# Differential attention in a two-block network: the work behind a tile's scores cut into three pieces that run over four steps

## The chip, the cores and the metric

The kernel runs on one core of a Trainium2 chip. The metric is the device time of one execution in microseconds. Everything is float32; the dense matrix products split each operand into a rounded high part and the rest (dtype `fp32r`) and take three products for one.

## The reference, cut to what matters

Two blocks of two layers each act on 512 tokens of width 1024 (the second block also on 256 context tokens). The part that the change touches is the differential attention of the second block, in both of its layers: 4 heads, two softmax maps per head over 768 keys (512 of the sequence, 256 of the context), subtracted with a learned factor, times the values, then a norm over each head.

```python
def diff_softmax_attend(q, keys, vals, lam):
    s = jnp.einsum('bqhmd,bkhmd->bhmqk', q, keys).astype(jnp.float32) * (DA_QK ** -0.5)
    p = jax.nn.softmax(s, axis=-1)
    w = p[:, :, 0] - lam * p[:, :, 1]
    return jnp.einsum('bhqk,bkhv->bqhv', w.astype(vals.dtype), vals)
...
def diff_out(o):
    return (rms_norm(o, da_subln) * (1.0 - lam_init)).reshape(o.shape[:2] + (DA_WIDTH,))
yl = jnp.concatenate([hgrn_out(ol_f + ol_b, pl[2]), diff_out(od_l).astype(hl.dtype),
                      fourier_mix(pl[8])], axis=-1) @ w_out
```

In the first of the two layers the context tokens attend too, over the 256 context keys alone; in the second only the 512 sequence tokens do. So a head has 6 query tiles of 128 tokens in layer 0 (two of them context tiles) and 4 in layer 1: 24 + 16 = 40 tiles of a head.

## The kernel before

The program is written for a tile framework. It tracks dependences between tiles, gives each tag of a pool a number of buffers, and puts the instructions of each engine into a fixed order when it compiles: the order in which the program issues them is the priority, but an instruction that the compiler finds not ready is passed by later ones. On the chip each engine works through that fixed order and waits where something is late.

`mixer` is the sequence mixer of a layer. Its last stage is the differential attention, loop over heads `h` and tiles `c` (`order`), with dense work spread in between. The dense work comes from a `Filler`: a chain of generators (projections of the second pair of heads, the gate projection, the Fourier branch, half of the output projection) that `fill.step(cols)` advances by about `cols` columns of matrix product (512 columns are one dense product). A step takes `DA_COLS` = 8000 (layer 0) or 7500 (layer 1) columns.

For each tile the program has two pieces:

- `diff_front` (L1418): for both maps, scores on TensorE into a PSUM tile `at` (L1431; 512 + 256 columns for a sequence tile, 256 for a context tile), row minimum on VectorE (L1434), exponential with row sum on ScalarE into a buffer `P` (L1436), then the two small terms (L1440, L1441) and the combined weights, written into the first map's buffer, on VectorE (L1442).
- `diff_back` (L1445): transposes of the combined weights on TensorE into PSUM tiles `tp`, 6 for a sequence tile (L1453); copies to `wT` on ScalarE, two for a sequence tile (L1454); the products with the values (L1460), two key blocks side by side in the array; a copy to `o2` on ScalarE (L1463); a small product with a stacked identity that adds the two halves (L1464); a scaled copy into `od` on ScalarE (L1465). Plain float32 products appear in the trace as two instructions each, so L1460 has 12 for a sequence tile and L1464 has 2.

A step of the loop issues `diff_front` of tile i, then `fill.step(DA_COLS[l])`, then `diff_back` of tile i-1. Tiles of the last head also get `attn_out` (L1603: square, reduce, norm, transposes L1588, split into the output projection's operands) one step after their `diff_back`. After the loop come three `fill.step(DA_LAST)` with the last pieces between them.

PSUM has 8 banks here: `acc` (dense products) 2 tiles of one bank, `tp` 2 tiles of one bank, `at` 2 tiles of two banks. `tp` is shared by the transposes, the value products, the Fourier branch (L1546) and L1588. `wT` and `o2` have 2 buffers, `P` has 5, `ard` (the factor 1/sum) 6 by its pool's default. The evacuation of a gate product is `gfn` (L1517: tanh on ScalarE L1519, product on VectorE L1520, product on GpSimd L1521). Weights come by DMA and are split by `wsplit` into `hi` on ScalarE (L288) and `lo` on VectorE (L289). The dense products are L301, L302, L305 (`mm_a_g`) and L321 to L323 (`mm_b_g`).

Of the kernel before, what the change touches and what calls it, by code (L numbers as in the profile page):

```python
# [9 lines left out]
F32 = mybir.dt.float32  # L10
# [3 lines left out]
AF = mybir.ActivationFunctionType  # L14
# [12 lines left out]
DA_COLS = (8000, 7500)  # L27
# [4 lines left out]
DA_LAST = 5832  # L32
DA_FIRST = 9540
# [218 lines left out]
class Builder:  # L252
# [1165 lines left out]
    def diff_front(self, p, l, maps, c):  # L1418

        nc = self.nc  # L1420
        N = T + CT
        k0 = 0 if c < 4 else T
        nk = N - k0
        P = []
        den = self.t(self.small, [128, 2], F32, "aden")
        for m in range(2):
            QS, KS = maps[m]
            ps = self.t(self.ps, [128, 1024], F32, "at")
            for o in range(k0, N, 512):
                n = min(512, N - o)  # L1430
                nc.tensor.matmul(ps[:, o - k0:o - k0 + n], lhsT=QS[:, 128 * c:128 * c + 128], rhs=KS[:, o:o + n],  # L1431
                                 start=True, stop=True)
            mx = self.t(self.small, [128, 1], F32, "amx")
            nc.vector.tensor_reduce(mx, ps[:, :nk], AX.X, ALU.min)  # L1434
            e = self.t(p, [128, N], F32, "P", NP)
            nc.scalar.activation(out=e[:, :nk], in_=ps[:, :nk], func=AF.Exp, scale=-1.0, bias=mx, accum_out=den[:, m:m + 1])  # L1436
            P.append(e)

        rd = self.t(self.small, [128, 2], F32, "ard")
        nc.vector.reciprocal(rd, den)  # L1440
        nc.vector.scalar_tensor_tensor(rd[:, 1:2], den[:, 0:1], self.lam[:, l:l + 1], rd[:, 1:2], ALU.mult, ALU.mult)  # L1441
        nc.vector.scalar_tensor_tensor(P[0][:, :nk], P[1][:, :nk], rd[:, 1:2], P[0][:, :nk], ALU.mult, ALU.add)  # L1442
        return P[0], rd, k0, nk

    def diff_back(self, p, h, c, front, dv, od):  # L1445
        nc = self.nc
        W, rd, k0, nk = front
        wT = self.t(p, [128, T + CT], F32, "wT", 2)
        for o in range(0, nk, 512):
            n = min(512, nk - o)  # L1450
            pt = self.t(self.ps, [128, 512], F32, "tp")
            for i in range(0, n, 128):
                nc.tensor.transpose(pt[:, i:i + 128], W[:, o + i:o + i + 128], self.ident)  # L1453
            nc.scalar.copy(wT[:, o:o + n], pt[:, :n])  # L1454

        po = self.t(self.ps, [128, 192], F32, "tp")
        nb = nk // 128
        for i in range(nb):
            g = 64 * (i % 2)
            nc.tensor.matmul(po[g:g + 64, :128], lhsT=dv[:, k0 // 128 + i, 64 * h:64 * h + 64], rhs=wT[:, 128 * i:128 * i + 128],  # L1460
                             start=(i < 2), stop=(i >= nb - 2), tile_position=(0, g))
        o2 = self.t(p, [128, 128], F32, "o2", 2)
        nc.scalar.copy(o2, po[:, :128])  # L1463
        nc.tensor.matmul(po[:, 128:], lhsT=o2, rhs=self.ident2, start=True, stop=True)  # L1464
        nc.scalar.activation(out=od[:, c, 64 * h:64 * h + 64], in_=po[:, 128:], func=AF.Copy, scale=rd[:, 0:1])  # L1465

    def mixer(self, l, hp, hT, hc, vx, vt, fill):

        nc, tc, A = self.nc, self.tc, self.A
        both = self.segs(hT, hc)  # L1470
        qseg = both if l == 0 else both[:1]
        W = A["wi_a"][l]
        nt = 6 if l == 0 else 4
        NQ = 128 * nt
# [3 lines left out]
        dv = self.t(mx, [128, 6, 256], F32, "dv")  # L1478

        ha, hb = ExitStack(), ExitStack()  # L1480
        if vt is None:
            vt, fill = self.scan_values(l, self.pool(vx, f"vx{l}", side="right"), both)
# [11 lines left out]
        fill = Filler(dense[1])  # L1494
        chains = {0: self.hgrn_chain(hg[0], hg[1], l, 0, vt, oh, NQ, *st[0])}
        h = 1
        while chains:
            for i, g in list(chains.items()):
                if next(g, "end") == "end":
                    chains.pop(i)  # L1500
                    if i == 2:
# [4 lines left out]
                        prep = [self.diff_prep(dp, W, both, NQ, j) for j in range(2)]  # L1506
# [8 lines left out]
        da = self.pool(ctx, f"da{l}")  # L1515
# [9 lines left out]
        br = {}  # L1525
# [77 lines left out]
        def attn_out(c):  # L1603
# [8 lines left out]

        fill = Filler(prep[1], self.dense_b_g([(A["wi_g"][l, i], (2, 512)) for i in range(4)], self.tok_tiles(qseg), gfn),
                      fourier(), out_half())
        pend = []
        for h in range(4):
            if h == 0:
                stacks = [self.diff_stack(da, i, NQ) for i in range(2)]
                fill.step(DA_FIRST)
            elif h < 3:  # L1620
                while fill.gens and fill.gens[0] is prep[1]:
                    fill.step(512)
                stacks.append(self.diff_stack(da, h + 1, NQ))
            maps = stacks[h]
            for c in order:
                fr = self.diff_front(da, l, maps, c)
                fill.step(DA_COLS[l])
                if pend:
                    self.diff_back(da, *pend[-1], dv, od)
                if h == 3 and len(pend) > 3 * nt + 1:  # L1630
                    while "l" not in br or (l == 0 and "c" not in br):
                        fill.step(512)
                    attn_out(pend[-2][1])
                pend.append((h, c, fr))
        fill.step(DA_LAST)
        self.diff_back(da, *pend[-1], dv, od)
        fill.step(DA_LAST)
        attn_out(order[-2])
        fill.step(DA_LAST)
        attn_out(order[-1])  # L1640
        fill.drain()
        brT, brc = br["l"], br.get("c")
        ctx.close()
# [309 lines left out]
```

## Time and profile before

| | |
|---|---|
| median of 3 runs | 2590.91 us (2587.81 to 2595.76) |
| the profiled execution, its own time | 2587.33 us |
| its span from first to last instruction | 2585.5 us |
| TensorE busy | 2511.3 us, 97% of the span |
| mean granted clock of TensorE | 0.993 |
| differential attention with its dense work, layer 0 | 1049 to 1205 us of the span |
| the same, layer 1 | 2043 to 2157 us of the span |

The profile is one execution. The span lies 1.8 us under that execution's own time, and that time 3.6 us under the median of the runs. PE is TensorE's matrix products, PEld its weight loads, which overlap them; DVE is VectorE, ACT ScalarE, POOL GpSimd. An engine's busy time is the union of its instructions; the products of PE are pipelined and overlap their neighbours, so the pace of PE is read from start to start, not from durations.

### The profile page before, as it was taken

Reading aid. Unit: us, or ns where it says so; the run is one execution under the profiler, and the core shown is the slowest. Engines: PE = TensorE matmul, PEld = TensorE weight load, DVE = VectorE, ACT = ScalarE, POOL = GpSimd, SP = SyncE. Lnnn points to the kernel's source line nnn. Section 1 sums busy time; section 2 is a strip of 40 time slices with the busy share of each in tenths; the row PEclk is TensorE's granted clock in tenths of the full one; section 3 lists DMA queues with packets and bytes.
Section 4 is the critical chain, followed back from the end, with each engine's and each line's share of the span. In section 5 each row is a group of like instructions: output and inputs, shape, how many; then the busy total and the mean of one; then the engine's idle time right before and its main releaser. Section 6 shows DMA issues by size and latency. Waiting matters only on the chain.

```text
span 2585.5 us, 38643 instructions
## 1 busy us (share of the span) xinstructions
PE 2511.3 (97%) x15587; PEld 2071.2 (80%) x15587; DVE 1516.8 (59%) x2502; ACT 1031.9 (40%) x1962; POOL 241.7 (9%) x288
## 2 busy tenths in 40 slices
PE   8999999999999999999999999999999999999997
PEld 7777887787777888777988888888788777887886
DVE  5657588645365577666756544445567766443434
ACT  6523333333444544465631211212655466522222
POOL 0000012102000000512100000000100412000001
PEclk9999999999999999999999999999999999999999
DMA  5424364342131211522543333332211434322222
GB/s 187 159 73 162 107 228 131 98 131 74 58 130 66 82 34 53 146 81 101 190 146 123 131 122 105 127 120 90 90 58 50 120 110 147 115 91 97 91 97 81
DMA packets 85169, 284.63 MB, mean 110 GB/s; under 512 B 12176, under 2 KB 15072, under 8 KB 84608
## 3 DMA queue, kind: packets, MB, share of 16 engines
q1 hardware_dynamic: 78880, 263.50, 30.0%
q0 software_dynamic: 4864, 15.74, 2.2%
q10 hardware_dynamic: 1248, 2.95, 0.4%
q8 instruction: 122, 2.00, 0.3%
q14 instruction: 55, 0.45, 0.1%
HBM read 253.78 MB, written 21.00 MB: 106 GB/s over the span
## 4 chain that ended last, share of the span: by engine, by line
PE 77%; DVE 7%; issue 5%; ACT 5%; DMA 3%; POOL 2%; SPq 0%; DVEq 0%; POOLq 0%; ACTq 0%
PE acc L301 13%; PE acc L305 13%; PE acc L302 13%; PE acc L321 9%; PE acc L323 9%; PE acc L322 9%; DVE lo L289 2%; ACT hi L288 1%; PE tp L1460 1%; PE at L1431 1%; DMA raw<-in_wo 1%; PE tp L1453 1%; ACT junk L344 1%; ACT hf L388 1%; PE at L650 1%
## 5 line engine op out<-in xcount | busy, mean ns | idle before, releaser
L289 DVE TENSOR_TENSOR lo<-raw,hi 128x1024 fp32r<-128x1024 f32 (+1 forms) x321 | 388.0, 1211 | 400.0 <-ACT hi L288 279.2
L288 ACT ACTIVATE hi<-raw 128x1024 fp32r<-128x1024 f32 (+1 forms) x321 | 335.9, 1048 | 559.2 <-PE acc L323 228.4
L301 PE MATMUL acc<-hTh,hi 128*128 128x512 f32 (+1 forms) x1408 | 547.6, 393 | 5.2 <-ACT hTh L565 2.7
L302 PE MATMUL acc<-hTl,hi 128*128 128x512 f32 (+1 forms) x1408 | 542.2, 389 | 0.3 <-DVE hTl L566 0.2
L305 PE MATMUL acc<-hTh,lo 128*128 128x512 f32 (+1 forms) x1408 | 352.0, 388 | 0.0
L321 PE MATMUL acc<-hi,hTh 128*128 128x512 f32 (+3 forms) x832 | 317.0, 383 | 5.9 <-ACT hi L288 2.4
L301 PEld LDWEIGHTS acc<-hTh,hi 128*128 128x128 f32 x1408 | 266.7, 190 | 65.3 <-issue 3.9
L322 PE MATMUL acc<-lo,hTh 128*128 128x512 f32 (+3 forms) x832 | 310.9, 374 | 2.9 <-DVE lo L289 2.6
L323 PE MATMUL acc<-hi,hTl 128*128 128x512 f32 (+3 forms) x832 | 311.2, 375 | 0.4 <-DVE hTl L566 0.4
L302 PEld LDWEIGHTS acc<-hTl,hi 128*128 128x128 f32 x1408 | 267.4, 190 | 54.7 <-DVE hTl L566 0.7
L305 PEld LDWEIGHTS acc<-hTh,lo 128*128 128x128 f32 x1408 | 254.8, 188 | 55.8 <-issue 0.2
L321 PEld LDWEIGHTS acc<-hi,hTh 128*128 128x128 f32 x832 | 157.1, 189 | 38.4 <-issue 6.6
L322 PEld LDWEIGHTS acc<-lo,hTh 128*128 128x128 f32 x832 | 157.7, 190 | 29.4 <-DVE lo L289 7.1
L323 PEld LDWEIGHTS acc<-hi,hTl 128*128 128x128 f32 x832 | 157.4, 189 | 27.6 <-DVE hTl L566 2.7
L321 PE MATMUL acc<-hi,ph 128*128 128x512 f32 x440 | 175.0, 398 | 0.0
L323 PE MATMUL acc<-hi,pl 128*128 128x512 f32 x440 | 173.8, 396 | 0.0
L322 PE MATMUL acc<-lo,ph 128*128 128x512 f32 x440 | 173.3, 394 | 0.0
L301 PE MATMUL acc<-hThc,hi 128*128 128x256 f32 x608 | 149.2, 283 | 0.0
L302 PE MATMUL acc<-hTlc,hi 128*128 128x256 f32 x608 | 148.0, 281 | 0.0
L433 DVE SCALAR_TENSOR_TENSOR bgraw<-bgraw,cb 128x1024 f32<-128x1024 f32 x96 | 117.1, 1219 | 17.7 <-DMA bgraw<-in_w_mod 16.7
L1791 DVE TENSOR_TENSOR y<-y,acc 128x512 f32<-128x512 f32 x112 | 76.5, 686 | 82.1 <-PE acc L323 81.7
L301 PEld LDWEIGHTS acc<-hThc,hi 128*128 128x128 f32 x608 | 114.4, 188 | 2.5
(340 smaller groups left out, 3697.8 us busy)
## 6 DMA issues: line engine op xcount, KB each, us to landing
bgraw<-in_w_mod SPq DMA_DIRECT2D x96, 512.0 KB, 3.3
raw<-in_wf_in SPq DMA_DIRECT2D x88, 512.0 KB, 3.3
raw<-in_wf_out SPq DMA_DIRECT2D x44, 512.0 KB, 3.3
raw<-in_wb_a SPq DMA_DIRECT2D x38, 512.0 KB, 3.8
raw<-in_wi_a SPq DMA_DIRECT2D x36, 512.0 KB, 3.3
raw<-in_wo SPq DMA_DIRECT2D x32, 512.0 KB, 3.5
xt<-xd SPq DMA_DIRECT2D x16, 512.0 KB, 3.6
raw<-in_wb_v SPq DMA_DIRECT2D x12, 512.0 KB, 3.4
```

What stands on the lines that cost most here:

```text
L288: nc.scalar.activation(out=hi[:, :n], in_=raw[:, :n], func=AF.Copy)
L289: self.pin = nc.vector.tensor_tensor(out=lo[:, :n], in0=raw[:, :n], in1=hi[:, :n].bitcast(F32), op=ALU.subtract)
L301: mm(ps, lhsT=wh[:, k], rhs=xh[:, k, n0:n0 + n], start=(k == 0), stop=False)
L302: mm(ps, lhsT=wh[:, k], rhs=xl[:, k, n0:n0 + n], start=False, stop=False)
L305: mm(ps, lhsT=wl[:, k], rhs=xh[:, k, n0:n0 + n], start=False, stop=(k == KT - 1))
L321: mm(ps, lhsT=xh, rhs=wh[:, j], start=(k == 0), stop=False)
L322: mm(ps, lhsT=xh, rhs=wl[:, j], start=False, stop=False)
L323: mm(ps, lhsT=xl, rhs=wh[:, j], start=False, stop=(k == nk - 1))
L344: self.nc.scalar.activation(out=junk[:, :x.shape[-1]], in_=x, func=AF.Square, accum_out=dst)
L388: nc.scalar.activation(out=hf[:, j], in_=ps[:, j], func=AF.Identity, scale=a[:, k:k + 1], bias=b[:, k:k + 1])
L433: nc.vector.scalar_tensor_tensor(out, raw, 1.0, cb[:, v], ALU.mult, ALU.mult, accum_out=md[:, v, k:k + 1])
L1791: nc.vector.tensor_tensor(out=ys[c][:, hs], in0=ys[c][:, hs], in1=ps, op=ALU.add)
```

## The change

`diff_back` is cut into `diff_keys` (transposes and copies to `wT`), `diff_values` (value products and the copy to `o2`) and `diff_end` (the small product and the copy into `od`). The loop runs over the tiles of all heads in one list. A step i now issues: `diff_keys` of tile i-1, `diff_front` of tile i, `diff_values` of tile i-2, `attn_out` of a tile of the last head whose `diff_end` was in the step before, `diff_end` of tile i-3, and then the dense work of the step. Three more steps at the end, with `DA_LAST` each, empty the chain. The last small product gets a `tp` tile of its own, so a sequence tile takes four of them where it took three. `ard` is asked for with 6 buffers by name.

```diff
-        rd = self.t(self.small, [128, 2], F32, "ard")
+        rd = self.t(self.small, [128, 2], F32, "ard", 6)
...
-    def diff_back(self, p, h, c, front, dv, od):
+    def diff_keys(self, p, front):
+
         nc = self.nc
-        W, rd, k0, nk = front
+        it, (P, rd, k0, nk) = front
         wT = self.t(p, [128, T + CT], F32, "wT", 2)
         for o in range(0, nk, 512):
             n = min(512, nk - o)
             pt = self.t(self.ps, [128, 512], F32, "tp")
             for i in range(0, n, 128):
-                nc.tensor.transpose(pt[:, i:i + 128], W[:, o + i:o + i + 128], self.ident)
+                nc.tensor.transpose(pt[:, i:i + 128], P[:, o + i:o + i + 128], self.ident)
             nc.scalar.copy(wT[:, o:o + n], pt[:, :n])
-
-        po = self.t(self.ps, [128, 192], F32, "tp")
+        return it, (wT, rd, k0, nk)
+
+    def diff_values(self, p, keys, dv):
+
+        nc = self.nc
+        (h, c), (wT, rd, k0, nk) = keys
+        po = self.t(self.ps, [128, 128], F32, "tp")
         nb = nk // 128
         for i in range(nb):
             g = 64 * (i % 2)
-            nc.tensor.matmul(po[g:g + 64, :128], lhsT=dv[:, k0 // 128 + i, 64 * h:64 * h + 64], rhs=wT[:, 128 * i:128 * i + 128],
+            nc.tensor.matmul(po[g:g + 64], lhsT=dv[:, k0 // 128 + i, 64 * h:64 * h + 64], rhs=wT[:, 128 * i:128 * i + 128],
                              start=(i < 2), stop=(i >= nb - 2), tile_position=(0, g))
         o2 = self.t(p, [128, 128], F32, "o2", 2)
-        nc.scalar.copy(o2, po[:, :128])
-        nc.tensor.matmul(po[:, 128:], lhsT=o2, rhs=self.ident2, start=True, stop=True)
-        nc.scalar.activation(out=od[:, c, 64 * h:64 * h + 64], in_=po[:, 128:], func=AF.Copy, scale=rd[:, 0:1])
+        nc.scalar.copy(o2, po)
+        return (h, c), (o2, rd)
+
+    def diff_end(self, values, od):
+
+        nc = self.nc
+        (h, c), (o2, rd) = values
+        po = self.t(self.ps, [128, 64], F32, "tp")
+        nc.tensor.matmul(po, lhsT=o2, rhs=self.ident2, start=True, stop=True)
+        nc.scalar.activation(out=od[:, c, 64 * h:64 * h + 64], in_=po, func=AF.Copy, scale=rd[:, 0:1])
+        return h, c
...
+        items = [(h, c) for h in range(4) for c in order]
+        front = keys = vals = done = None
+        for i in range(len(items) + 3):
+            h, c = items[i] if i < len(items) else (None, None)
...
+            keys, vals, ends = front and self.diff_keys(da, front), keys, vals
+            front = h is not None and ((h, c), self.diff_front(da, l, stacks[h], c))
+            vals = vals and self.diff_values(da, vals, dv)
+            if done:
+                while "l" not in br or (l == 0 and "c" not in br):
                     fill.step(512)
...
+                attn_out(done[1])
+            done = ends and self.diff_end(ends, od)
+            if done and done[0] < 3:
+                done = None
+            fill.step(DA_COLS[l] if h is not None else DA_LAST)
+        attn_out(done[1])
         fill.drain()
```

## Rows read from the trace of the kernel before

**Rows 1.** The page: busy time by engine, and the chain that ended last by engine.
```profile
PE 2511.3 (97%) x15587; PEld 2071.2 (80%) x15587; DVE 1516.8 (59%) x2502; ACT 1031.9 (40%) x1962; POOL 241.7 (9%) x288
...
PE 77%; DVE 7%; issue 5%; ACT 5%; DMA 3%; POOL 2%; SPq 0%; DVEq 0%; POOLq 0%; ACTq 0%
```
**Rows 2.** Stretches: length, busy time of PE, PEld, DVE, ACT, POOL, clock, DMA.
```profile
1049.00:1205.00 156.00, 148.81 (x952) 118.44 (x953) 104.36 (x198) 94.31 (x239) 33.75 (x52) 1.00 0.28 87
2043.00:2157.00 114.00, 106.28 (x679) 82.39 (x678) 80.77 (x134) 71.58 (x164) 35.08 (x59) 0.97 0.36 106
```
**Rows 3.** Waits of the weight loads (PEld), layer 0's stage: us, times, longest.
```profile
PEld tp L1460 <- ACT wT L1454: 8.4, 22, 1.3
...
PEld tp L1464 <- ACT o L1463: 1.4, 4, 0.7
PEld tp L1453 <- ACT wT L1454: 1.4, 2, 1.1
...
PEld tp L1453 <- DVE P L1442: 0.2, 1, 0.2
```
**Rows 4.** The same view, layer 1's stage.
```profile
PEld tp L1460 <- ACT wT L1454: 4.8, 15, 0.5
...
PEld tp L1464 <- ACT o L1463: 1.3, 4, 0.7
```
**Rows 5.** PE in order of time, a step of layer 1: start, us, line, operation, count.
```profile
2076.37 0.82 PE L1453 MATMUL tp<-ident,P 128*128 128x128 f32 x6
2076.94 0.83 PE L1431 MATMUL at<-KS,QS 128*128 128x512 f32 x3
2077.70 0.88 PE L1460 MATMUL tp<-wT,dv 128*64 128x128 f32 x12
...
2078.73 0.39 PE L321 MATMUL acc<-hi,hTh 128*128 128x512 f32 x1
2078.96 0.40 PE L322 MATMUL acc<-lo,hTh 128*128 128x512 f32 x1
2079.19 0.33 PE L1464 MATMUL tp<-ident,o 128*128 128x64 f32 x2
2079.33 0.48 PE L323 MATMUL acc<-hi,hTl 128*128 128x512 f32 x1
...
2082.46 0.82 PE L1453 MATMUL tp<-ident,P 128*128 128x128 f32 x6
```
**Rows 6.** PE, then PEld, in order of time, inside a step of layer 0.
```profile
1085.68 0.40 PE L321 MATMUL acc<-hi,hTh 128*128 128x512 f32 x1
1086.12 0.88 PE L1460 MATMUL tp<-wT,dv 128*64 128x128 f32 x12
1086.92 0.50 PE L322 MATMUL acc<-lo,hTh 128*128 128x512 f32 x1
1087.26 0.40 PE L323 MATMUL acc<-hi,hTl 128*128 128x512 f32 x1
...
1086.12 0.64 PEld L1460 LDWEIGHTS tp<-wT,dv 128*64 128x64 f32 x12 [0.36 <-ACT wT L1454]
```
**Rows 7.** DVE in order of time: the combined weights of the scores in Rows 5.
```profile
2081.41 1.02 DVE L1442 SCALAR_TENSOR_TENSOR P<-P,ard,P 128x768 f32<-128x768 f32 x1
```
**Rows 8.** Stretches as in Rows 2: small products alone, PE idle, the time after.
```profile
1099.55:1109.46 9.91, 7.65 (x70) 5.72 (x68) 8.12 (x14) 8.06 (x22) 0.03 (x1) 1.00 0.01 2
2099.00:2101.00 2.00, 0.00 (x0) 0.00 (x1) 1.88 (x3) 1.06 (x3) 0.00 (x0) 0.98 0.50 195
2101.00:2103.00 2.00, 2.00 (x5) 1.61 (x6) 2.00 (x3) 1.15 (x3) 1.97 (x3) 0.50 0.78 256
```
**Rows 9.** PE: the first product after the idle stretch of Rows 8.
```profile
2101.00 0.80 PE L301 MATMUL acc<-hTh,hi 128*128 128x512 f32 x1 [2.46 <-DVE gth L1520]
```
**Rows 10.** ACT in order of time, a weight split in layer 1's stage.
```profile
2098.04 1.05 ACT L288 ACTIVATE hi<-raw 128x1024 fp32r<-128x1024 f32 x1
```
**Rows 11.** PE: the last transposes of `attn_out` in layer 0.
```profile
1204.54 0.38 PE L1588 MATMUL tp<-ident,od 128*128 128x128 f32 x2
```

More of the change, by code (lines that the diff above doesn't have):

```diff
@@ L1614, in mixer @@
                       fourier(), out_half())
[L1615 to L1621, printed above, removed]
-                    fill.step(512)
[L1623 to L1640, printed above, removed]
+        items = [(h, c) for h in range(4) for c in order]
+        front = keys = vals = done = None
+        for i in range(len(items) + 3):
+            h, c = items[i] if i < len(items) else (None, None)
+            if c == order[0]:
+                if h == 0:
+                    stacks = [self.diff_stack(da, j, NQ) for j in range(2)]
+                    fill.step(DA_FIRST)
+                elif h < 3:
+                    while fill.gens and fill.gens[0] is prep[1]:
+                        fill.step(512)
+                    stacks.append(self.diff_stack(da, h + 1, NQ))
+            keys, vals, ends = front and self.diff_keys(da, front), keys, vals
[3 more added lines that the diff above has]
+                while "l" not in br or (l == 0 and "c" not in br):
+                    fill.step(512)
+                attn_out(done[1])
[4 more added lines that the diff above has]
+        attn_out(done[1])
         fill.drain()
```

## The prediction

> **What bounds the kernel now.** Start with the page: TensorE is busy for 97% of the span, VectorE for 59%, ScalarE for 40%, and the chain that ended last is 77% TensorE [rows 1]. A change that leaves all products in place, as this one does, can win only where PE waits or restarts. Next come the windows over the two attention stages [rows 2]: in layer 0 PE is busy 148.81 of 156.00 us, in layer 1 106.28 of 114.00, so 14.9 us are openly idle; modelled ends hide some more. Then the waits [rows 3, 4]. The weight loads stand still most often in front of the value products, until ScalarE has copied the transposed weights: 8.4 us in 22 waits and 4.8 us in 15, so in 37 of 40 tiles. Before the small identity product they wait for its copy, 1.4 + 1.3 us. Last, the order of PE in two steps. In one [rows 5] transposes, scores, value products come with no dense product between them, then two dense products at a pace of 0.23 us (2078.73 to 2078.96), the identity product, and dense work to the end of the step at 6.09 us (2076.37 to 2082.46). In the other [rows 6] the compiler put one dense product into the gap before the value products, and that one took 0.44 us from its start to the next (1085.68 to 1086.12) instead of 0.23: 0.21 us lost, while the weight load showed 0.36 us idle. So 0.58 us of PE goes with each 1 us of idle weight load; the rest lies behind a product that is still running.
>
> Note what the first of these steps says: the small products already stand together there, since the compiler reorders. There little is to be had.
>
> **The change, part by part.** No instruction is added or removed on any engine; the products, copies and evacuations are the same. What moves:
>
> *Value products one step behind their copies.* The 37 waits go, as the copies are made a step, some 6 us, earlier: (8.4 + 4.8) x 0.58 = 7.7 us of PE.
>
> *Identity product one step behind its copy.* (1.4 + 1.3) x 0.58 = 1.6 us.
>
> *Fewer restarts.* The first dense product behind the value products takes 0.34 us to the next one (1086.92 to 1087.26) instead of 0.23, 0.11 more [rows 6]. Of the two steps shown one has this and the other has a score product there, so I take 20 of 40 tiles: 2.2 us (0 to 4.4). The restart behind the identity product (0.48 us long at 2079.33 against 0.40 [rows 5]) stays, once a step, and is neither won nor lost.
>
> Together 7.7 + 1.6 + 2.2 = 11.5 us.
>
> *Transposes one step earlier.* This is the cost. Before, the program asks for a tile's transposes after the dense work of the following step; now at the start of that step, right behind one portion of dense work. They need the combined weights, which come out of a chain over VectorE and ScalarE (minimum, two exponentials, sums, combination). Take the step of [rows 5]: its first score product starts at 2076.94, the combination starts at 2081.41 and lasts 1.02 us [rows 7], so the weights are ready at 2082.43, 5.49 us later, and the next step's first transpose starts at 2082.46. In the old order that transpose belongs to the tile before and has a whole step to spare: in layer 0 a transpose waits for the combination once, for 0.2 us [rows 3]. In the new order it is this tile's own, with 0.03 us to spare. Anything that enters the chain, a weight split of 1.05 us on ScalarE [rows 10] for example, makes it late, and behind a late transpose on PE stand the scores of the next tile, the value products and all dense work of the step. What helps is that the compiler sees most of this and may put scores and dense products in front. What is left is its misjudgement, and the nearest row for one is what it let happen at the value products: 13.2 us over 37 waits, 0.36 us each of load, 0.21 of PE. From below the price is 0; at 0.21 us for each of the 32 sequence tiles it is 6.7 us. Since the margin is 0.03 us, nearer to waiting than to not, I take two thirds: 4.5 us.
>
> *Four `tp` tiles a step through two buffers, not three.* Transposes already wait 1.4 us for a buffer in layer 0 [rows 3]. The identity product no longer holds the tile of the value products, but takes one of its own. Either sign, 1.4 us at most; I take 0.
>
> *The rest* costs nothing: `ard` had 6 buffers already; `wT` and `o2` hold two tiles at once and have two buffers; each combined-weights buffer is held no longer than before. The stacks' DMAs on GpSimd's queue stand at the same place of the program. `attn_out` comes about two tiles later in the loop, but at the end both orders have three portions of dense work and then the rest of the output projection; in layer 0 its last transposes run at 1204.54 of a stage in which dense work goes on behind them [rows 11]. Without that cover its chain over three engines would show once a layer.
>
> Sum: 11.5 - 4.5 = 7.0 us won. The profiled execution, 2587.33 us with 1.8 us around its span, would become 2580.3; it lies 3.6 us under the median of the runs, which would become 2590.9 - 7.0 = 2583.9. About 0.3%, 7.8 us, is what a measurement of this kernel can tell from no change, and the forecast is just inside.
>
> **A rule on the clock that speaks against it.** In the stretch from 1099.55 to 1109.46 PE did nothing but transposes, scores, value and identity products, busy 7.65 of 9.91 us, and its granted clock stayed at 1.00. After 2 us with no product at all it fell to 0.50, the lower of its two levels of 1.2 and 2.4 GHz [rows 8]. The Trainium skill, in "TensorE: Matmul & The Clock Gate", Part 4 on transposes, says that the full clock does not engage for transposes. By that rule bundles of small products could end at the lower level. The trace does not bear it out for this mix of products, so the rule gets 2 in 100.
>
> **The rivals.** *Late transposes* (the other side). PE stops at the head of most bundles until VectorE has combined the weights. It decides from 11.5 / 32 = 0.36 us of PE per sequence tile on: beyond that the change loses, and from 0.60 us on it is measurably slower. A weight split of 1.05 us caught in half the tiles gives 16 x 1.05 = 16.8 us, net 5 lost: 2596; in 24 tiles 25 us, net 14 lost: 2605. For it: the margin of 0.03 us. Against it: the compiler's filling. Chance 0.20, with about 2600.
>
> *It changes nothing.* The compiler's order decides, and it bundles already [rows 5]; with late copies its dense fill moves elsewhere and meets the same misjudgement at the transposes, 11.5 us won and as much returned, give or take 4: 2587 to 2594. Chance 0.25.
>
> *More than its own waits.* The stretches without dense work are broken up as well: 2.26 us idle of the 9.91 [rows 8], 2.46 us in front of 2101.00, where a dense product waited for a gate's evacuation [rows 9], and the time at clock 0.50 behind it, which does in 2 us the work of 1. With those 5.7 us and the full 11.5 the time is 2574. Chance 0.15: PE would have to find other work while ScalarE is behind, and the gate's evacuations are not moved.
>
> *The clock falls after each bundle.* If the dense work ran at 0.50 for 2 us in each of 40 steps, 40 us would be lost against 11.5 won: 2619. Chance 0.02.
>
> **How the numbers follow.** The forecast itself has 0.38, with 2584 and a range of its own from 2579 (all 11.5 won) to 2590 (the 6.7 returned and no restart saved, 11.5 - 2.2 - 6.7 = 2.6 won, and a little more). The bound lies at 2583.1, so it splits about evenly, 0.20 faster and 0.18 same. Faster: 0.20 + 0.15 and 0.05 of the no-change case, 0.40. Same: 0.18 + 0.18 from no change and 0.02 from late transposes, 0.38. Slower: 0.18 from late transposes, 0.02 from no change and 0.02 from the clock, 0.22. For 8 in 10 the range reaches from the case below, 2572, to the late transposes at 2602.
>
> **What would show it.** Right: the waits of L1460 for L1454 and of L1464 for L1463 nearly vanish from the weight loads; a step's PE order is transposes, scores, value and identity products, dense; the two stages together shrink by about 7 us. Wrong: a wait of L1453 for L1442 of over 0.3 us in most tiles (late transposes), dense products still standing between the small ones (no change), a clock under 1.00 behind bundles, or longer stretches without dense products while a gate waits on ScalarE. A gain or loss outside the two stages would mean that the compiler's order moved elsewhere, which I count at nothing.

## The result, and the profile after

The changed kernel takes 2607.99 us (median of 6 runs, 2603.4 to 2609.8), the kernel before 2594.47 us in the same session (2587.81 to 2599.41): a ratio of 1.0056, 95% interval 1.0044 to 1.0067. That is slower by some 14.5 us by the ratio (13.5 between the two medians). The forecast was 7.0 us faster, and its range ended at 2602. The same kernel run again later gave 1.0061 (1.0048 to 1.0074).

The page of the changed kernel, busy time and chain, against [rows 1]: PE is busy 2.7 us longer in a span that is 16.1 us longer (2601.6 against 2585.5).

```profile
PE 2514.0 (97%) x15587; PEld 2073.0 (80%) x15587; DVE 1518.6 (58%) x2502; ACT 1032.0 (40%) x1962; POOL 239.4 (9%) x288
...
PE 75%; DVE 7%; ACT 6%; issue 6%; DMA 4%; POOL 2%; SPq 0%; POOLq 0%; DVEq 0%; ACTq 0%
```

The two attention stages of the changed kernel, then the last head's end in each (columns as in [rows 2]). The stages, with ends set by eye, are 10 and 4.5 us longer than in [rows 2], with 13.32 and 12.98 us idle on PE and not 7.19 and 7.72:

```profile
1050.00:1216.00 166.00, 152.68 (x956) 120.29 (x956) 105.42 (x199) 95.31 (x239) 33.71 (x52) 0.99 0.26 79
2052.50:2171.00 118.50, 105.52 (x679) 83.21 (x679) 81.82 (x134) 71.47 (x164) 34.00 (x58) 0.97 0.35 102
...
1190.00:1216.00 26.00, 22.42 (x136) 16.47 (x134) 14.16 (x34) 11.96 (x30) 6.06 (x6) 1.00 0.06 21
2140.00:2171.00 31.00, 26.62 (x178) 20.87 (x179) 21.88 (x44) 17.28 (x42) 4.05 (x4) 1.00 0.06 18
```

The idle time of these two ends, 3.58 and 4.38 us, is a handful of waits of PE. In layer 0 it is five waits of `attn_out`'s transposes. In layer 1 it is three of them (2.57 us), one of a tile's transposes for the combined weights (1.29) and one of the value products behind it (0.51). In the kernel before, the ends had 0.37 and 0.70 us of it (in shorter windows, as they hold less work):

```profile
1192.00:1205.00 13.00, 12.63 (x83) 9.76 (x82) 4.87 (x14) 5.43 (x14) 3.02 (x3) 1.00 0.05 20
...
2142.00:2157.00 15.00, 14.30 (x90) 10.84 (x89) 8.76 (x22) 7.80 (x21) 4.80 (x4) 1.00 0.00 1
```

The waits of the weight loads in layer 0's stage, against [rows 3] (the value products are now L1466, the copy to `wT` L1455, the identity product L1477, `attn_out`'s transposes L1602). The 22 waits that were to vanish are 17, and four before the identity product end with a copy of transposes too; new are 4.7 us in front of L1602:

```profile
PEld tp L1466 <- ACT wT L1455: 7.0, 17, 1.1
PEld tp L1602 <- issue: 4.7, 4, 1.4
PEld tp L1477 <- ACT wT L1455: 2.2, 4, 1.3
```

Layer 1's stage, against [rows 4]: 15 waits before, 13 now.

```profile
PEld tp L1466 <- ACT wT L1455: 4.7, 13, 0.8
```

The waits of PE itself, whole kernel. The third row is the feared one, transposes that wait for the combined weights: once.

```profile
PE tp L1602 <- DVE od L1624: 6.1, 8, 1.0
...
PE acc L301 <- DVE gth L1534: 5.0, 1, 5.0
...
PE tp L1454 <- DVE P L1442: 1.3, 1, 1.3
```

Before, L301 waited 2.5 us for the gate [rows 9], and the transposes of `attn_out` (L1588 there) 1.1 us for `od`:

```profile
PE tp L1588 <- DVE od L1610: 1.1, 3, 0.4
```

**A steady step.** PE in the changed kernel, the step that answers to [rows 5]:

```profile
2085.69 0.82 PE L1454 MATMUL tp<-ident,P 128*128 128x128 f32 x6
2086.26 0.94 PE L1431 MATMUL at<-KS,QS 128*128 128x512 f32 x4
2087.14 0.88 PE L1466 MATMUL tp<-wT,dv 128*64 128x128 f32 x12
2087.94 0.43 PE L1477 MATMUL tp<-ident,o 128*128 128x64 f32 x2
...
2091.76 0.51 PE L1431 MATMUL at<-KS,QS 128*128 128x512 f32 x2
```

The small products do come together, and 15 dense products follow. The step takes 6.07 us (2085.69 to 2091.76); before it took 6.09. The weight load of the value products waits here, 0.25 us, exactly as long as in the step of [rows 5]:

```profile
2087.13 0.64 PEld L1466 LDWEIGHTS tp<-wT,dv 128*64 128x64 f32 x12 [0.25 <-ACT wT L1455]
```

In the trace of before the row of that load is this one:

```profile
2077.69 0.64 PEld L1460 LDWEIGHTS tp<-wT,dv 128*64 128x64 f32 x12 [0.25 <-ACT wT L1454]
```

Both waits lie behind scores that are still streaming, so neither costs PE anything. And the new one can't be for the data: these products read weights that were copied a step ago. What the copy of this step's transposes sets free is one of the two `tp` buffers.

**The last head's end, layer 0.** All engines, `attn_out` of two tiles:

```profile
1193.80 0.33 PE L1477 MATMUL tp<-ident,o 128*128 128x64 f32 x2
...
1194.61 0.91 ACT L1436 ACTIVATE P<-at,amx 128x768 f32<-128x768 f32 x1
...
1196.08 0.42 ACT L1619 ACTIVATE P<-od 128x256 f32<-128x256 f32 x1
...
1198.77 0.43 DVE L1624 TENSOR_TENSOR od<-od,ors 128x256 f32<-128x256 f32 x1 [1.12 <-POOL ors L339]
...
1199.35 0.41 PE L1602 MATMUL tp<-ident,od 128*128 128x128 f32 x2 [0.68 <-DVE od L1624]
...
1199.59 0.33 PE L1477 MATMUL tp<-ident,o 128*128 128x64 f32 x2
...
1200.16 0.31 ACT L1478 ACTIVATE od<-tp,ard 128x64 f32<-128x64 f32 x1
...
1200.50 0.42 ACT L1619 ACTIVATE P<-od 128x256 f32<-128x256 f32 x1
...
1201.66 1.01 POOL L339 TENSOR_TENSOR ors<-rsv,cm 128x4 f32<-128x4 f32 x1 [2.92 <-DVE rsv L338]
1202.70 0.43 DVE L1624 TENSOR_TENSOR od<-od,ors 128x256 f32<-128x256 f32 x1 [1.12 <-POOL ors L339]
...
1203.27 0.41 PE L1602 MATMUL tp<-ident,od 128*128 128x128 f32 x2 [0.53 <-DVE od L1624]
```

Read it as a ring. The identity product at 1199.59 makes `od`; six small operations on three engines later, at 1203.13 (1202.70 + 0.43), the normed `od` is there: 3.54 us. PE has some 3.1 us of other work between (1199.59 to 1203.27, less 0.53), reaches the transposes and stands still. The next tile's identity product is queued right behind them, so the next chain starts late as well. The chain is not always that short. Behind the identity product at 1193.80 ScalarE had an exponential (L1436) and part of a copy to `wT` to do before the square (L1619), and the chain took 5.40 us (to 1199.20). There PE waited 0.68 us although it had 4.87 us of other work.

In the kernel before, the distance from identity product to transposes was 7.08 us for the last tile but one and 4.42 for the last (to 1204.54 [rows 11]), behind chains of 3.3 us:

```profile
1195.14 0.33 PE L1464 MATMUL tp<-ident,o 128*128 128x64 f32 x2
...
1200.12 0.33 PE L1464 MATMUL tp<-ident,o 128*128 128x64 f32 x2
...
1202.22 0.38 PE L1588 MATMUL tp<-ident,od 128*128 128x128 f32 x2
...
1203.03 0.42 DVE L1610 TENSOR_TENSOR od<-od,ors 128x256 f32<-128x256 f32 x1 [1.12 <-POOL ors L339]
```

Over both layers three of the ten tiles' transposes waited before, and eight wait now.

The compiled order of PE shows why, layer 0's end (T transposes of weights, S scores, V value products, I identity product, F transposes of `attn_out`, D dense, with counts of products in the program):

```
before  I1 D4 F2 D3 T4 S3 T2 V6 S1 D5 I1 D1 F2 D9 T6 D2 V6 F2 D1 I1 D9 T6 D2 V6 D2 I1 D8 F2 D9 F2
after   F2 I1 D4 T4 D2 T2 D1 V6 D5 F2 I1 D3 T6 D2 V6 F2 D1 I1 D4 V6 D4 F2 I1 D10 F2 I1 D12 F2
```

**Where the 16.1 us lie.** Each trace was cut at the points where PE had done the same products as the trace of before at 1045, 1190, 1240, 2040, 2140 and 2190 us; the table shows the lengths minus those of before (145.1, 50.0, 99.9, 50.1 us). A difference of 1 us or so can come from where a cut falls, and the columns "heads" take in the first tiles of the last head (in layer 0 it starts near 1158 us).

```
kernel                        heads L0   end L0   heads L1   end L1
changed                         +4.9      +3.5      +0.4      +5.1
changed, second execution       +6.7      +3.7      +1.4      +3.7
```

The remaining 2.2 us lie outside the stages. So both the heads and the end lose, and the experiments take them one by one.

### The profile page after: what moved, and what is told of

It reads as the page before. It is cut to its first block, busy times and chain, and to the rows that moved or that the text cites. A ratio compares the mean times of both kernels' runs of the same rounds, so it can differ in the third digit from the quotient of the medians.

```text
span 2601.6 us, 38640 instructions
## 1 busy us (share of the span) xinstructions
PE 2514.0 (97%) x15587; PEld 2073.0 (80%) x15587; DVE 1518.6 (58%) x2502; ACT 1032.0 (40%) x1962; POOL 239.4 (9%) x288
## 4 chain that ended last, share of the span: by engine, by line
PE 75%; DVE 7%; ACT 6%; issue 6%; DMA 4%; POOL 2%; SPq 0%; POOLq 0%; DVEq 0%; ACTq 0%
PE acc L305 13%; PE acc L301 13%; PE acc L302 12%; PE acc L321 9%; PE acc L323 9%; PE acc L322 9%; DVE lo L289 2%; ACT hi L288 2%; DMA raw<-in_wo 1%; PE tp L1466 1%; PE at L1431 1%; PE tp L1454 1%; PE at L1289 1%; ACT junk L344 1%; PE tp L684 1%
## 5 line engine op out<-in xcount | busy, mean ns | idle before, releaser
L301 PE MATMUL acc<-hTh,hi 128*128 128x512 f32 (+1 forms) x1408 | 547.4, 393 | 7.8 <-DVE gth L1534 5.0
L301 PEld LDWEIGHTS acc<-hTh,hi 128*128 128x128 f32 x1408 | 266.8, 190 | 67.3 <-DVE gth L1534 5.4
L301 PE MATMUL acc<-hThc,hi 128*128 128x256 f32 x608 | 149.1, 282 | 0.0
L301 PEld LDWEIGHTS acc<-hThc,hi 128*128 128x128 f32 x608 | 114.5, 188 | 2.6
```

The source lines that it names most:

```text
L301: mm(ps, lhsT=wh[:, k], rhs=xh[:, k, n0:n0 + n], start=(k == 0), stop=False)
```

## The experiments

The theories, as the expectations name them. END: the loss is made behind the last head. BUFFER: the small products wait for one of two `tp` buffers, and the change has a fourth `tp` tile a step. LATE TRANSPOSES: the rival of the prediction. All runs are timed against the kernel before in the same session (2590.31 us for `e2`, `e4`, `e5` and `e6`; 2590.73 for `e3`, `e7`, `e9` and `e10`; 2590.31 for `e1`, `e8`, `e11` and `e12`; 2589.78 for `e0` and `e13` to `e15`). The diffs are abridged.

### Which half loses

`e4_old_last_head`: heads 0 to 2 in the new order, last head and end as before; where the order changes, the pieces of two tiles that are still due are issued at once. `e5_new_last_head`: the reverse. The diff is that of `e4`.

```diff
 for i, (h, c) in enumerate(items):
+    if h < 3:
         keys, vals, ends = front and self.diff_keys(da, front), keys, vals
         ...
+        continue
+    last, front = front, ((h, c), self.diff_front(...))
+    fill.step(DA_COLS[l]); back(last); attn_out(two tiles back)
```

> Heads 0 to 2 in the new order, the last head and what follows it as in the kernel before. Theory END (the loss is made behind the last head, where the attn_out calls now fall two tiles later, among the three last dense portions): the loss of 13.5 us shrinks by about 9 to 4 to 5, so some 2598 us. Theory BUFFER (the small products wait for one of the two tp buffers all through the heads, one tp tile more a step): three quarters of the loss stay, some 2604 us. Theory LATE TRANSPOSES (they wait for the combined P): as BUFFER, some 2604 us.

> The opposite half: heads 0 to 2 as in the kernel before, the last head and what follows it in the new order. Theory END: some 9 us slower than before, 2603 us. Theory BUFFER and theory LATE TRANSPOSES: a quarter of the loss, 3 us, some 2597 us. If the losses of this run and of the other half add up to 13.5, nothing else is in it.

Measured: 2595.46 us, ratio 1.0018 (1.0009 to 1.0026), and 2599.68 us, 1.0030 (1.0019 to 1.0041). The end alone costs some 7.8 us, the heads some 4.7; together 12.5, within the intervals all of the loss. END is most of it, but not all. In the trace of `e5` the ring stands as in the change, in layer 0 to 0.01 us; its 5.2 us are 4.1 more than before, of the 7.8:

```profile
PE tp L1602 <- DVE od L1624: 5.2, 8, 0.9
```

### What it is at the end

`e2_attn_same_step` puts each `attn_out` directly behind the tile's identity product, `e1_end_first` puts the identity product ahead of the `attn_out` of the tile before it, `e3_more_last` moves dense work from the heads to the end, `e12_late_attn` is the kernel before with `attn_out` alone two tiles later, and `e13_attn_later` is the changed kernel with it one more step later.

```diff
 e1   -if done: attn_out(done[1])
      -done = ends and self.diff_end(ends, od)
      +late, done = done, ends and self.diff_end(ends, od)
      +if late: attn_out(late[1])
 e2   +done = ends and self.diff_end(ends, od)
      +if done and done[0] == 3: attn_out(done[1])
 e3   -DA_COLS = (8000, 7500); DA_LAST = 5832
      +DA_COLS = (7729, 7094); DA_LAST = 8000
 e12  -if h == 3 and len(pend) > 3 * nt + 1: attn_out(pend[-2][1])
      +if h == 3 and len(pend) > 3 * nt + 3: attn_out(pend[-4][1])
 e13  -done = ends and self.diff_end(ends, od)
      +late, done = done, ends and self.diff_end(ends, od)     # attn_out(late[1]) a step later
```

> The changed kernel with each tile's attn_out right behind its diff_end, one step earlier than in the change. Theory END: the place of attn_out decides; the waits of its transposes for od (12 us in both layers) are still there where too little work stands between the end and them, but one portion fewer is at stake: 4 to 9 us of the 13.5 come back, 2599 to 2604 us. If the transposes now wait for the whole chain behind od in the same step (about 4 us for each of 10 tiles), it is slower than the changed kernel by up to 20 us, and then the chain's length and not its step is what counts. Theories BUFFER and LATE TRANSPOSES: 2608 us, as the changed kernel.

> The changed kernel with the identity product of a tile ahead of attn_out of the tile before it, and not behind it; nothing else moved. If the loss of the end comes from the identity product queued behind the transposes: the chain from od to the transposes of the next step starts about 1 us earlier for each of 10 tiles, and 3 to 6 of the 8 us come back, 2600 to 2604 us. If lateness of attn_out itself costs: 2607 us, as the changed kernel, within 1.5 us.

> The changed kernel with the dense portions behind the last head 8000 columns long and not 5832, and the portions of the heads shorter by as much in all (7729 and 7094 and not 8000 and 7500). Theory END: the transposes of attn_out have 0.9 us more of dense work ahead of them in each of three portions of two layers, so up to 5 us come back, 2602 to 2605 us, less what the shorter portions of the heads cost. Theories BUFFER and LATE TRANSPOSES: the waits of the heads stay or grow, 2608 us or more.

> The kernel before, its pipeline untouched, with attn_out alone two tiles later, as in the change: four calls behind the last head with three dense portions. Theory END by lateness itself: 6 to 8 us slower than before, as with the new last head alone. If the cut into pieces is what costs (the identity product of the next tile stands behind the transposes of attn_out, so each tile's od comes late), then lateness alone costs 0 to 2 us, since here od of a tile is done long before.

> The changed kernel with attn_out one more step later: its transposes stand two portions behind the identity product that makes their od, and not one. Theory DISTANCE (what costs at the end is not that attn_out is late, but that in the new order too little work stands between a tile's identity product and its attn_out transposes, less than the some 4 us of the chain over three engines): moved later still, it gets faster, 5 to 8 us come back, 2597 to 2602 us by a kernel before of 2590.5. If the loss of the end is that of three tiles' pieces behind the last scores: nothing comes back, 2604 us or more.

Measured, in the order of the texts above: `e2` 2606.77 us, 1.0061 (1.0049 to 1.0073); `e1` 2605.01 us, 1.0051 (1.0039 to 1.0063); `e3` 2602.20 us, 1.0045 (1.0033 to 1.0057); `e12` 2589.92 us, 0.9995 (0.9987 to 1.0004); `e13` 2600.96 us, 1.0046 (1.0033 to 1.0058).

`e12` is the clearest: four `attn_out` behind the last head, as late as in the change, cost nothing when each `od` is ready before them: here they stand 4.9 to 17.3 us behind the identity products. In its trace PE waits for `od` at no transpose. Lateness by itself is not the cause. `e13` points the same way, and its time lies in the range of theory DISTANCE. Moved later still, the change is faster by 3.9 us against its own second run (1.0061 to 1.0046) and by 2.6 against the first (1.0056), but the intervals overlap, so this gain is not shown by the times. The wait that was 6.1 us in 8 is

```profile
PE tp L1602 <- DVE od L1624: 1.9, 2, 1.0
```

and one more of 0.83 us at 1200.43, which the view puts down to a later operation of VectorE: 3.4 us less in all. But 11.9 us of loss stay, of which the heads make 4.7: at the end some 7 are left, give or take several by the intervals. Of these the trace shows the 2.7 us of L1602 and 1.8 us in layer 1, transposes that wait for the combined weights (1.28) with the value products behind them (0.51). The rest is open.

`e2` makes the distance shorter. Its wait grows to

```profile
PE tp L1602 <- DVE od L1624: 9.2, 9, 2.7
```

and yet its time can't be told from the changed kernel's. `e3` makes the distance longer and shortens the end (in its trace the ends are 0.9 and 3.1 us over before and not 3.5 and 5.1), but its heads grow by 11.2 and 4.1 us. In layer 0 some 17 us of them ran at a granted clock of 0.50. Its median lies in END's range, its interval overlaps that of the changed kernel. For `e1` 3 to 6 us were expected and 1 to 3 came (against 1.0056 and 1.0061), less than can be told: in its compiled order of layer 0 the last three tiles have 8, 12 and 13 dense products between I and F, in the change 8, 10 and 12. The compiler had its own say on the place of I, and the wait sank only from 6.1 to 3.3 us.

### The tp buffers

`e6_shared_tp` is the changed kernel with one `tp` tile for both small products of a step; `e8_old_order_4tp` the kernel before with a tile of its own for the identity product; `e9_values_first` turns the changed step round (V, I, scores, T, dense), so that no product stands behind a copy of its own step; `e10_vf_old_last` does so with the old end, and `e11_vf_old_last_3tp` adds the shared tile.

```diff
 e6   -po = self.t(self.ps, [128, 128], F32, "tp")  ...  po = self.t(self.ps, [128, 64], F32, "tp")
      +po = self.t(self.ps, [128, 192], F32, "tp")     # once a step; V in :128, I in 128:
 e8   -nc.tensor.matmul(po[:, 128:], lhsT=o2, ...)
      +pe = self.t(self.ps, [128, 64], F32, "tp")
      +nc.tensor.matmul(pe, lhsT=o2, ...)
 e9   -keys, vals, ends = front and self.diff_keys(da, front), keys, vals
      +vals, ends = keys and self.diff_values(da, keys, dv), vals
       ...                                              # attn_out, diff_end, diff_front
      +keys = last and self.diff_keys(da, last)
```

> The changed kernel with one tp tile a step for the value product and the identity product together, as the kernel before had, so three tp tiles a step and not four. Theory BUFFER: the identity product waits for no buffer any more and the value products still for one; of the waits of the body 2 to 5 us come back, 2603 to 2606 us. Theory END and theory LATE TRANSPOSES: as the changed kernel, 2608 us, within 1.5 us.

> The kernel before, its order untouched, with a tp tile of its own for the identity product, so four tp tiles a step as in the change. If the fourth tile makes the loss of the heads: 3 to 5 us slower than before, 2594 to 2596 us by the kernel before of the last job. If the new order itself makes it: as before, within 1.5 us.

> The changed kernel with the order of a step turned round: first the value products of the tile before last and the identity product, then the scores, and the transposes of the last tile at the end of the step, before the dense portion. The same lag and the same four tp tiles, but no product of a step stands behind the copy of transposes of the same step. Theory BUFFER: most of the 11.7 us that the value products' weight loads wait for a tp buffer go, 5 to 8 us come back, 2599 to 2603 us. Theory LATE TRANSPOSES: they now have the scores ahead of them as well, so their waits go too; the same, but the waits that go would be those of the transposes. Theory END alone: 2607 us, as the changed kernel.

> The turned order in heads 0 to 2, the last head and what follows it as in the kernel before. If the end costs 8 us and the buffer waits of the body some 5 or more, both losses go: 2586 to 2592 us, at or just under the kernel before. If only the end is to blame, 2595 us, as with the changed order in heads 0 to 2.

> The turned order in heads 0 to 2 with the last head as before, and one tp tile a step for both small products. If the fourth tile costs what is left of the loss of this form (3 us): level with the kernel before or 1 to 2 us under it, 2589 to 2591 us. If not: 2593 to 2594 us, as with four tiles.

Measured: `e6` 2605.68 us, 1.0054 (1.0042 to 1.0066); `e8` 2591.33 us, 1.0005 (0.9996 to 1.0013); `e9` 2601.97 us, 1.0048 (1.0032 to 1.0064); `e10` 2593.74 us, 1.0013 (1.0005 to 1.0022); `e11` 2598.92 us, 1.0030 (1.0018 to 1.0042).

The fourth tile costs nothing (`e8`), and sharing it back wins nothing that can be told (`e6`, `e11`). The medians of `e6` and `e9` lie in the ranges of theory BUFFER, but their intervals overlap those of the changed kernel, so they decide nothing; `e4` against `e10`, with 11 runs each, is the better test. The traces of `e6`, `e9` and `e11` lost 3 to 4 us near 305 us, at half clock, in a stage that is the same in all kernels, so that their last few microseconds say little; that `e11` is slower than `e10` is left open. BUFFER names the waits rightly and is wrong on their price: from `e4` to `e10`, which differ by the turned order alone, the waits of the value products' loads go from

```profile
PEld tp L1466 <- ACT wT L1455: 11.0, 28, 1.1
PEld tp L1466 <- issue: 2.2, 9, 0.4
```

to

```profile
PEld tp L1466 <- ACT wT L1455: 6.2, 16, 0.9
PEld tp L1466 <- issue: 5.7, 17, 0.4
```

and the time by 0.0005, some 1.3 us, less than the intervals. Load waits here are mostly cover, not loss; some of them only change the name of what ends them.

### Late transposes, and the pieces one by one

`e7_scores_first` issues a step's scores ahead of the transposes. `e14_end_alone` defers only the identity product, `e15_keys_later` has all three pieces in three steps, but each a tile later, so that the transposes are asked for where the kernel before has them; both keep the old end. `e0_after_again` is the changed kernel itself.

```diff
 e7   -keys, ... = front and self.diff_keys(da, front), ...; front = ... self.diff_front(...)
      +last, front = front, ... self.diff_front(...); keys, ... = last and self.diff_keys(da, last), ...
 e14  +vals_new = self.diff_values(da, self.diff_keys(da, last), dv)   # as before, behind the portion
      +if vals: self.diff_end(vals, od)                               # of the tile before
 e15  +front = self.diff_front(...); fill.step(DA_COLS[l])
      +keys, vals, ends = last and self.diff_keys(da, last), keys, vals; diff_values; diff_end
```

> The changed kernel with the scores of a step ahead of the transposes, and the value and identity products behind these. Theory LATE TRANSPOSES: the transposes have some 2 us of scores more ahead of them, and their waits go: 4 to 7 us come back, 2601 to 2604 us. Theory BUFFER: the value products now stand directly behind the copies of the transposes, with no scores between: more wait for the buffer, 2608 to 2614 us. Theory END: 2607 us, as the changed kernel.

> In heads 0 to 2 the identity product alone goes to the next tile's step; transposes and value products stay where the kernel before has them; the last head is as before. If the transposes being asked for a step earlier make the loss of the heads (some 3 to 5 us): level with the kernel before, 2590 to 2592 us. If the standing together of value products and identity product makes it: 2593 to 2596 us. In neither case is a gain of over 2 us expected.

> In heads 0 to 2 the three pieces of the change in three steps, but each a tile later: the transposes are asked for where the kernel before has them, behind the dense portion of the next step. The last head is as before. If the earlier transposes make the loss of the heads: level with the kernel before, 2590 to 2592 us. If the cut into pieces makes it: 2593 to 2596 us.

> The changed kernel itself, in the job of the others. All theories: 1.0056 of the kernel before, 2605 us. Its profile tells which of the small differences inside the heads come back in a second execution, the stretch at half clock at 1170 us above all: if it comes back at the same place, it belongs to the order; if not, to the execution.

Measured: `e7` 2607.44 us, 1.0064 (1.0051 to 1.0077); `e14` 2596.63 us, 1.0026 (1.0017 to 1.0035); `e15` 2593.89 us, 1.0014 (1.0005 to 1.0023); `e0` 2605.23 us, 1.0061 (1.0048 to 1.0074).

LATE TRANSPOSES falls as the main cause: scores ahead of them bring nothing, and PE waits for the combined weights once (1.3 us, at 2151.25 in the last head of layer 1). `e15` keeps the old place of the transposes and is level with `e4` (1.0018), `e14` loses 6.7 us with the identity product alone moved. All five kernels with a new order in the heads and the old end (`e4`, `e10`, `e11`, `e14`, `e15`) lose 3.4 to 7.8 us; both with the old order in all heads (`e8`, `e12`) lose nothing. So the heads' loss goes with the order. All five send the identity product to a later step, and `e14`, which moves nothing else, loses already. No run keeps it in its place and moves the other pieces, so which piece it takes is not shown.

The traces say where it starts. There is one stretch in layer 0 without dense products [rows 8]. In the old order T, S, V and I of neighbouring tiles fill each other's gaps there. In the new one seven score products stand in a row and wait for the exponentials to free `at`. This is the changed kernel, the stretch and then PE inside it; the stretch of [rows 8] had 7.65 us busy of 9.91, this has 6.52 of 10.09:

```profile
1101.43:1111.52 10.09, 6.52 (x51) 4.48 (x50) 8.00 (x14) 7.45 (x19) 0.16 (x1) 1.00 0.01 2
...
1102.30 0.62 PE L1431 MATMUL at<-KS,QS 128*128 128x512 f32 x2 [0.27 <-ACT P L1436]
1104.11 0.62 PE L1431 MATMUL at<-KS,QS 128*128 128x512 f32 x2 [1.19 <-ACT P L1436]
1105.10 0.50 PE L1431 MATMUL at<-KS,QS 128*128 128x512 f32 x1 [0.37 <-ACT P L1436]
```

The granted clock stayed at 1.00 there in both executions of the changed kernel and in `e4`. In `e13`, whose PE order is the same up to the last head and which has the same gaps of 1.19 and 0.37 us, it fell to 0.50, the lower of the two levels, in a slice of 1.5 us with 1.09 us without a product (the same slice of the changed kernel has 1.11 and stayed at 1.00):

```profile
1103.00:1104.50 1.50, 0.41 (x2) 0.30 (x2) 1.46 (x5) 1.46 (x3) 0.00 (x0) 1.00 0.00 0
1104.50:1106.00 1.50, 1.13 (x7) 0.86 (x6) 1.50 (x4) 0.52 (x2) 0.00 (x0) 0.89 0.00 0
1106.00:1107.50 1.50, 1.47 (x11) 1.17 (x11) 0.80 (x3) 1.25 (x3) 0.00 (x0) 0.50 0.00 0
```

and in `e14`, whose transposes wait 1.33 us for the combined weights at this place, dense work behind the stretch ran at the lower level as well:

```profile
1112.00:1113.50 1.50, 1.50 (x10) 1.07 (x7) 0.00 (x0) 0.57 (x3) 1.50 (x2) 0.50 0.00 0
1113.50:1115.00 1.50, 1.50 (x5) 1.21 (x4) 0.69 (x1) 0.49 (x2) 0.32 (x2) 0.50 0.47 139
```

A fall between 1104 and 1117 us is in the profiles of `e1`, `e2`, `e3`, `e13` and `e14`, none with the old order there. In layer 1 the gate's wait of [rows 9] is 4.9 to 5.3 us in the changed kernel, `e2`, `e4`, `e6` and `e13`, 3.3 in `e15`, and 2.5 in `e5` and `e14`. The half clock at 1170 us came back in the second execution of the changed kernel, longer (10.2 us and not 3.4), but `e8` and `e12` have one near 1165 too (3.4 us each), so it comes in either order, at the end of the Fourier branch. These are places; that they add up to the 4.7 us is not shown, since the single pieces are no larger than the difference between two executions.

The mean granted clock of whole executions says how much of the loss can be the clock's. It was 0.9907 and 0.9912 in the two groups of runs of the changed kernel, and 0.9926 to 0.9931 for the kernel before in the sessions of the experiments. That is some 10 us more at the lower level in each execution; as 2 us there do the work of 1, it is worth at most some 5 us (an estimate). For `e4` and `e5` (0.9922 and 0.9923 against 0.9926) it is at most 1 us each, so the losses of 4.7 and 7.8 us are not made by the clock. For `e14` (0.9908 against 0.9931) it is up to 6 of its 6.7 us.

## Why the prediction was wrong

**The first term, 7.7 us won at the value products: not there.** It took the 37 load waits of [rows 3, 4] and priced them at 0.58 of PE, from the one step of [rows 6], where a dense product stood in the gap. In a steady step the load waits 0.25 us behind scores that still run, before and after, and the step goes from 6.09 to 6.07 us. PE's own waits, a view that the prediction did not use, put the loss of the kernel before at the value products at 2.0 us in 4 waits, and the change has 2.4:

```profile
PE tp L1460 <- ACT wT L1454: 2.0, 4, 0.9
...
PE tp L1466 <- ACT wT L1455: 2.4, 4, 0.9
```

And the waits did not even vanish (30 of them are left), because a `tp` buffer and no longer the weights sets them. That the compiler spreads the three pieces anyway stood in the prediction ("There little is to be had"); the sum was made without it. The 1.6 us at the identity product and the 2.2 us of restarts are no more visible in the step.

**The price, 4.5 us for late transposes: hardly paid.** There is one wait of 1.3 us, with 0.5 us of the value products behind it, and `e7` shows that moving the transposes behind the scores brings nothing. The compiler's filling was named as what helps; in the step shown it put two score products ahead of the next transposes (2091.76). The rival of that name gave about 2600 us, and up to 2605, near the result. That is luck, as its waits did not come.

**The fourth `tp` tile, 0: right** (`e8`, 1.0005).

**"The rest costs nothing": the step that failed worst.** It counted three dense portions behind the last head in both orders, and named the cover without which the chain of `attn_out` "would show once a layer". It did not work out the distance from each identity product to its transposes. This shrank from 7.08 and 4.42 us to 3.68 in the stretch shown, against a chain of 3.54 us, and in a ring, so that the chain showed five times in layer 0 and three times in layer 1: 6.1 us of waits and not 1.1. The end costs 7.8 us (`e5`). `e12` shows that lateness by itself costs nothing; that more distance brings back 3 to 4 us is what the waits of `e13` say, while its time is not clear of noise. In the trace of the changed kernel the two ends are 8.6 us longer; 5.0 us of it are these waits and 1.8 the late transposes of layer 1 with what stands behind them. The rest is open.

**The rival that changes nothing** was right on the mechanism in the heads, that the compiler's order decides. It was not priced for a loss: 4.7 us in the heads (`e4`). That they come from an order that leaves worse gaps where no dense work is at hand is argued from the traces, and stays open in its parts.

**The clock.** The Trainium skill, "TensorE: Matmul & The Clock Gate", Part 4, has it that the full clock does not engage for transpose-mode products. The trace does not bear it out for this mix of products: the stretch at 1101.43 with its transposes stayed at 1.00 in two executions. The same order with the same gaps fell to 0.50 in a third, so neither the transposes nor the gaps alone decide, and what does is not shown. By the mean clock, the additional falls are worth at most some 5 us and not the 40 of that rival.

In sum, with the halves from `e4` and `e5`: 11.5 us did not come, 4.5 were not paid, 7.8 and 4.7 were lost: 7.0 + 12.5 = 19.5 of the 21.5 us between forecast (7.0 faster) and result (14.5 slower).

## What to carry to other kernels

Before a wait of the weight load is counted as time, look whether PE itself stands still there; if a product is still running, removing the wait gives nothing. When a pipeline is cut into more steps, work out for every consumer the distance from its producer in PE's compiled order, at the end above all, where the filling is short: a chain of 3.3 us over three engines was free behind 4.4 us of products, one of 3.5 us cost 0.5 to 1.0 us behind some 3, and where ScalarE was busy the chain took 5.4 us and 4.9 us of products did not hide it. Moving the consumer later can help and not hurt: in the old order it cost nothing, in the new one it took 3.4 us off the waits.

## What the hardware showed that was not expected

The granted clock is not a property of the order alone: the same instructions on PE between 1101 and 1111 us, behind the same gaps, ran at 1.00 in two executions and at 0.50 for some 3 us in a third. A weight load that waits for a buffer and one that waits for data look the same in the view of waits; only the order of the products, and which copy they read, tells them apart.
